# Three edits to a hybrid decoder layer: small column operations moved between engines, a load issued earlier, a sum of squares moved to VectorE

## The chip, the cores and the metric

The kernel runs on one core of one Trainium2 chip. The time is device microseconds of one execution; of several runs the median is taken. A core has a matrix engine (TensorE, PE in the profile, with its weight loads in a row of their own, PEld) and three engines for elementwise work, each with its own stream of instructions that it works off in order: VectorE (DVE), ScalarE (ACT) and GpSimd (POOL). SyncE (SP) issues nearly all DMA transfers here, also in order. PE writes to banks of PSUM; the program lets PE overwrite one only when it has been read.

## The reference

One decoder layer over x of 1024 tokens by 1024 columns, float32. What is computed, in short:

```python
h = rmsnorm(x, norm_g)
proj = h @ w_in     # gla q, k, v, gate, rank-16 code; stick-breaking q, k, v, gate; merge logits
log_a = log_sigmoid(g_rank @ w_dec_up + b_dec) / 16
# gated linear attention, 4 heads, in chunks of 64 tokens
attn = einsum(qe, ke) * mask;  o_intra = attn @ v
o = q_i @ S;  S = d_i[..., None] * S + k_i.T @ v_i        # scan over the chunks
y_a = (rmsnorm(o_gla, gla_norm_g) * silu(g_gate)) @ w_pa
# stick-breaking attention, 8 heads, queries in blocks of 128
A[t, s] = sigmoid(z[t, s]) * prod_{s<j<t} (1 - sigmoid(z[t, j]))
y_b = ((A @ v) * silu(s_gate)) @ w_pb
merged = g_a * y_a + g_b * y_b                            # g = sigmoid(m_logits + b_gate)
x = rmsnorm(x + merged @ w_o, final_g)
```

Both the inputs and the output are float32.

## The kernel before

**Products.** Each float32 operand of a large product is split into a high and a low part (tiles of type fp32r), and a product is made of three matmuls (high by high, low by high, high by low). `split` (L163 to L165) does this: ScalarE copies the high part (L164), VectorE subtracts it from the operand to get the low part (L165). Every large product also follows a scheme with seven block products instead of eight. `pair_job` (L235 on) does so for 256 columns of a weight: POOL makes sums of weight blocks (L243 to L246), `two` and `b22` split them, and the units 0 to 6 (L279 on) run one block product each, 12 matmuls at L269 to L271. After units 0, 2 and 3 `keep` (L275, ScalarE) copies the bank to a tile `f`; after the others an `evict` takes the result of a quarter (J, n): `total` (L308, VectorE) adds the kept tile to the bank. Units 0, 2 and 4 write to one bank in turn, each adding to what stands there, so the next product into it waits for the copy.

**Order of the work.** The program goes through these stages: (1) the start: row blocks of 128 tokens are normed, transposed on PE, and multiplied with the first weights of the values, which come in two halves of 512 rows; (2) the linear-attention values; (3) a list of pair jobs (merge gates, GLA q and k, gates, stick-breaking q, k, values), the later ones interleaved with the gated linear-attention recurrence, four units for each step; (4) stick-breaking attention; (5) the output products and the last norm, row block by row block. Engine orders are set by a scheduler, except within regions under `manual_schedule`, where ScalarE and VectorE follow the order of the code; the start (L483 on) and the last row are of this kind.

**The lines around the change.**

- The start: `norm_a(tb)` (L434) sums the squares of a row block on ScalarE (L438), multiplies by 1/1024 on VectorE (L229) and takes the power -1/2 on POOL (L230). L494 and L499 make the high part `hi0` and the low part `lo0` of the first weight half on VectorE; L500 makes the high part `hi1` of the second on ScalarE. `first_v` multiplies block 0 by them (L222); `turn_x` transposes the next block (L472) and splits it.
- The value pairs: `sv_pair` makes the stick-breaking values with tokens along the free axis. It needs the differences of neighbouring tokens. `vend` (L594) keeps the last token's column of each block of 128; `diff` subtracts 511 columns at once (L602) and the first column by itself, from `vend` of the half before (L604), or as a negation in the first half (L606). `turn` then transposes the differences on PE (L611), splits them and stores them (L615).
- The recurrence: steps are (head, block). `gl_half` loads `qe` and `ke` for four blocks (L894, L895); `gl_load` loads a step's values `vr` (L904) and its gate `g` (L906); `gl_local` makes the step's local attention and splits `vr` into `vh` and `vl`; `gl_gate` transposes the normed output (L970), multiplies by the gate and stores it. The tiles `vr` and `g` have three buffers each.
- The last row block comes in two halves of 256 columns. Each half adds its bank to `y` (L1589); ScalarE squares and sums it (L1591). For the first half the sum is added to that of the other 512 columns (L1595); for the second half both are added and scaled (L1598), POOL takes the power (L1599), and the row is scaled (L1602, L1603) and stored by two queues (L1605, L1606).

Of the kernel before, what the change touches and what calls it, by code (L numbers as in the profile page):

```python
# [9 lines left out]
F32 = mybir.dt.float32  # L10
# [92 lines left out]
def hybrid_layer(ctx: ExitStack, tc: tile.TileContext, x, norm_g, w_in, w_up, b_dec,  # L103
# [306 lines left out]
    with tc.tile_pool(name="p0", bufs=3, reuse_waits="tile") as p0:  # L410
# [70 lines left out]
        with tc.manual_schedule(engines={mybir.EngineType.Activation, mybir.EngineType.DVE}):  # L481
# [13 lines left out]
            keep_warm(WARM[1])  # L495
            for g in range(2):
                nc.vector.tensor_sub(hq[0, g][1][:, :, 0:P], pts[g], hq[0, g][0][:, :, 0:P].bitcast(F32))
            norm_a(1)
            nc.vector.tensor_sub(lo0, raw0, hi0.bitcast(F32))  # L499
            nc.scalar.activation(hi1, raw1, AF.Copy)  # L500
            for g in range(2):
                whole(0, g, pts[g])
# [79 lines left out]
    def sv_pair(i):  # L582


        held = []

        def evict(J, n, bank, add):
            if add is None:
                add = ev.tile([P, HALF], F32, tag="f", name="f")
                nc.scalar.activation(add, bank, AF.Copy)  # L590
            else:
                total(bank, add)
            h = 2 * i + J
            nc.vector.tensor_copy(vend[:, h, 4 * n:4 * n + 4], add[:, P - 1:HALF:P])  # L594
            held.append((J, n, h, add))
            if (J, n) != (1, 1):
                while held:
                    diff(*held.pop())

        def diff(J, n, h, add):  # L600
            d = ev.tile([P, HALF], F32, tag="f", name="f")
            nc.vector.tensor_sub(d[:, 1:HALF], add[:, 0:HALF - 1], add[:, 1:HALF])  # L602
            if n:
                nc.vector.tensor_sub(d[:, 0:1], vend[:, h, 3:4], add[:, 0:1])  # L604
            else:
                nc.vector.tensor_scalar(d[:, 0:1], add[:, 0:1], -1.0, None, op0=ALU.mult)  # L606

            def turn():
                pt = ps.tile([P, HALF], F32, tag="tr", name="tr")
                for b in range(4):  # L610
                    nc.tensor.transpose(pt[:, b * P:(b + 1) * P], d[:, b * P:(b + 1) * P], ident)  # L611
                o = stage()
                split(pt, o[:, 0], o[:, 1])
                for e in range(2):
                    nc.sync.dma_start(d_v[h][:, 4 * n:4 * n + 4, e],  # L615
                                      o[:, e].bitcast(F32).rearrange("p (b c) -> p b c", c=P))

            late.append(turn)

        return pair_job(w_in, C_SV + i * DV, evict)  # L620
# [245 lines left out]
    am = [gv.tile([P, P], F32, tag=f"am{i}", name=f"am{i}", bufs=1) for i in range(2)]  # L866
    for a in am:
        nc.gpsimd.memset(a[CH:P, 0:CH], 0.0)
    gh, ghalf, gblk = {}, {}, {}
    steps = [(h, b) for h in range(GLA_H) for b in range(NT)]  # L870

    def split2(src, shape, tag, bufs=2):
# [16 lines left out]
    def gl_half(h, m):  # L889
# [8 lines left out]
                             .unsqueeze(2).to_broadcast([P, 8, CH]))  # L898
        ghalf[h, m] = {"qe": qe, "q2": q2, "ke": ke}

    def gl_load(h, b):

        v = gv.tile([P, DV], F32, tag="vr", name="vr", bufs=3)
        nc.sync.dma_start(v, d_gv[:, b, h * DV:(h + 1) * DV])  # L904
        g = gv.tile([P, 2, P], F32, tag="g", name="g", bufs=3)
        nc.sync.dma_start(g, d_gg[h][:, :, b * P:(b + 1) * P])  # L906
        gblk[h, b] = {"vr": v, "g": g}
# [70 lines left out]
            nc.sync.dma_start(d_ogl[e][:, :, h, b * P:(b + 1) * P], o[:, :, e].bitcast(F32))  # L978

    gl_half(0, 0)  # L980
    gl_load(*steps[0])
    pairs.run(4)
    gl_load(*steps[1])
# [601 lines left out]
    for i in range(2):  # L1585
# [2 lines left out]
        product(bank, "A22", "T4", 3, i == 1, cs)  # L1588
        nc.vector.tensor_add(y[:, cs], bank[:, cs], y[:, cs])  # L1589
        junk = ps.tile([P, HALF], F32, tag="av", name="junk", bufs=1)  # L1590
        nc.scalar.activation(junk[:, cs], y[:, cs], AF.Square, accum_out=sq[:, i:i + 1])  # L1591
        if i == 0:
            for e in late:
                evict_c(*e)
            nc.vector.tensor_add(sq[:, 2:3], sq[:, 0:1], pre[1, 3][:, 0:1])  # L1595
            nc.vector.tensor_mul(y[:, cs], y[:, cs], fg[:, cs])
        else:
            nc.vector.tensor_scalar(r, sq[:, 1:2], sq[:, 2:3], 1.0 / D, op0=ALU.add, op1=ALU.mult)  # L1598
            nc.gpsimd.tensor_tensor(r, r, nhalf, op=ALU.pow)  # L1599
            nc.vector.tensor_mul(y[:, cs], y[:, cs], fg[:, cs])  # L1600
    cut = 5 * P
# [29 lines left out]
```

## Time and profile before

| what | value |
|---|---|
| median of 3 runs | 1177.04 us (1176.06 to 1178.81) |
| the profiled execution | 1176.68 us, span 1175.0 us |
| mean granted TensorE clock | 0.998 |
| memory read and written | 150.06 MB and 88.08 MB, 203 GB/s over the span |
| PE busy, 0 to 20 us (start) | 16.31 of 20 |
| PE busy, 20 to 280 us (values, first pair jobs) | 260.00 of 260 |
| PE busy, 280 to 300 us (recurrence begins) | 19.30 of 20 |
| PE busy, 300 to 700 us | 399.98 of 400 |
| PE busy, 700 to 720 us (a value pair) | 19.00 of 20 |
| PE busy, 720 to 1160 us | 439.53 of 440 |

A timeline row has the start in us, the duration in us, the engine, the line, the operation, the tile written and the tiles read, their shapes, and in brackets the idle time of the engine before it and what ended that. In a row of groups x is the count, then come the summed busy us and the mean ns of one. In a row of waits stand who waits for whom, and then the summed us of waiting, the number of waits and the longest one. A row of a DMA issue ends with the KB of one transfer and the us from its issue to its landing. In a window row each engine's busy us come in the order PE, PEld, DVE, ACT, POOL, then the granted clock, the DMA share and GB/s.

### The profile page before, as it was taken

What the parts mean: (1) busy time and instruction counts of PE and PEld (TensorE: products, weight loads), DVE (VectorE), ACT (ScalarE), POOL (GpSimd) and SP (SyncE); (2) the same over time, 40 slices, a digit from 0 to 9 for tenths busy, and PEclk for the clock granted to TensorE, in tenths of its full rate; (3) what the DMA queues carried; (4) which work ended last, traced back from release to release, by engine and by line L of the source; (5) the groups of instructions that cost most, each with busy time, mean ns of one, the idle gap of its engine ahead of it and who ended that gap; (6) DMA issues with size and microseconds to landing.
All of it is one profiled execution on the core that took longest, in us unless ns stands there. A gap on an engine that the chain in (4) does not pass through costs nothing.

```text
span 1175.0 us, 16650 instructions
## 1 busy us (share of the span) xinstructions
PE 1162.1 (99%) x5823; PEld 979.5 (83%) x5823; DVE 857.2 (73%) x1441; ACT 558.3 (48%) x1046; POOL 244.3 (21%) x217
## 2 busy tenths in 40 slices
PE   8999999999999999999999999999999999999997
PEld 8999888887888888888888888888888888888886
DVE  6797667888676876776666677457677876488986
ACT  6556663433444545544444343344444444365544
POOL 1022232334242242342242233000000000700001
PEclk9999999999999999999999999999999999999999
DMA  8325549997455665654444357799766656858652
GB/s 290 127 63 162 206 165 327 329 308 241 134 185 180 195 217 162 201 178 133 159 141 131 109 174 237 260 311 337 250 200 216 205 167 195 284 162 286 215 197 108
DMA packets 189456, 239.25 MB, mean 204 GB/s; under 512 B 12438, under 2 KB 128300, under 8 KB 187836
## 3 DMA queue, kind: packets, MB, share of 16 engines
q1 hardware_dynamic: 188796, 237.20, 61.1%
q8 instruction: 46, 0.75, 0.3%
q10 hardware_dynamic: 576, 0.98, 0.2%
q14 instruction: 38, 0.31, 0.1%
HBM read 150.06 MB, written 88.08 MB: 203 GB/s over the span
## 4 chain that ended last, share of the span: by engine, by line
PE 96%; DVE 2%; DMA 1%; ACT 1%; issue 1%; SPq 0%; POOLq 0%; POOL 0%; ACTq 0%; DVEq 0%
PE pp L269 17%; PE pp L270 17%; PE pp L271 17%; PE pp L204 3%; PE pp L205 3%; PE pp L203 3%; PE pp L222 2%; PE av L1108 2%; PE av L1109 2%; PE tr L1086 1%; PE av L1107 1%; PE z L1068 1%; PE z L1070 1%; PE z L1069 1%; PE xa L1363 1%; PE xa L1362 1%
## 5 line engine op out<-in xcount | busy, mean ns | idle before, releaser
L269 PE MATMUL pp<-S,wh 128*128 128x512 f32 x372 | 147.0, 395 | 0.7 <-ACT f L275 0.7
L271 PE MATMUL pp<-S,wl 128*128 128x512 f32 x372 | 145.0, 390 | 0.0
L270 PE MATMUL pp<-S,wh 128*128 128x512 f32 x372 | 144.9, 390 | 0.0
L308 DVE TENSOR_TENSOR f<-pp,f 128x512 f32<-128x512 f32 x93 | 63.9, 687 | 70.2 <-PE pp L271 63.8
L165 DVE TENSOR_TENSOR wl<-tt,wh 128x1024 fp32r<-128x1024 f32 x62 | 75.8, 1222 | 52.6 <-ACT wh L164 52.3
L164 ACT ACTIVATE wh<-tt 128x1024 fp32r<-128x1024 f32 x62 | 65.6, 1059 | 75.0 <-PE pp L270 67.4
L243 POOL TENSOR_TENSOR tt<-raw 128x512 f32<-128x512 f32 x31 | 43.5, 1403 | 258.8 <-DVE wl L165 232.8
L275 ACT ACTIVATE f<-pp 128x512 f32<-128x512 f32 x93 | 55.0, 592 | 79.8 <-PE pp L271 74.2
L1074 DVE TENSOR_TENSOR_SCAN be<-be,m 128x128 f32<-128x128 f32 (+3 forms) x64 | 86.1, 1347 | 3.4 <-ACT be L1071 3.2
L164 ACT ACTIVATE wh<-raw 128x1024 fp32r<-128x1024 f32 (+1 forms) x47 | 48.4, 1030 | 84.0 <-PE pp L270 48.5
L269 PEld LDWEIGHTS pp<-S,wh 128*128 128x128 f32 x372 | 70.5, 190 | 15.1 <-ACT f L275 0.9
L271 PEld LDWEIGHTS pp<-S,wl 128*128 128x128 f32 x372 | 69.8, 188 | 14.8
L270 PEld LDWEIGHTS pp<-S,wh 128*128 128x128 f32 x372 | 69.9, 188 | 13.8
L165 DVE TENSOR_TENSOR wl<-raw,wh 128x1024 fp32r<-128x1024 f32 (+1 forms) x47 | 63.1, 1343 | 18.4 <-ACT wh L164 17.2
L1071 ACT ACTIVATE be<-z 128x384 f32<-128x384 f32 (+4 forms) x96 | 47.2, 494 | 42.7 <-PE z L1070 38.2
L230 POOL TENSOR_TENSOR r<-r,nhalf 128x1 f32<-128x1 f32 x40 | 25.2, 629 | 194.3 <-DVE r L229 194.3
L1268 POOL TENSOR_TENSOR N<-A,A 128x512 f32<-128x512 f32 x4 | 6.6, 1660 | 241.0 <-DMA A<-d_osb 241.0
L269 PE MATMUL pp<-ha11h,wh 128*128 128x512 f32 x124 | 49.2, 397 | 0.0
L269 PE MATMUL pp<-ha12h,wh 128*128 128x512 f32 x124 | 49.0, 395 | 0.0
L164 ACT ACTIVATE dh<-raw 128x512 fp32r<-128x512 f32 x31 | 19.6, 631 | 61.4 <-PE pp L270 61.4
L269 PE MATMUL pp<-ha22h,wh 128*128 128x512 f32 x124 | 48.7, 393 | 0.0
L269 PE MATMUL pp<-S,dh 128*128 128x512 f32 x124 | 48.6, 392 | 0.0
(546 smaller groups left out, 3428.0 us busy)
## 6 DMA issues: line engine op xcount, KB each, us to landing
raw<-in_w_in_dram SPq DMA_DIRECT2D x31, 1024.0 KB, 6.2
d_t<-t SPq DMA_DIRECT2D x16, 512.0 KB, 4.8
d_ogl<-o SPq DMA_DIRECT2D x64, 128.0 KB, 2.4
d_q<-o SPq DMA_DIRECT2D x16, 512.0 KB, 3.3
d_k<-o SPq DMA_DIRECT2D x16, 512.0 KB, 4.8
d_v<-o SPq DMA_DIRECT2D x32, 256.0 KB, 2.3
k<-d_k SPq DMA_DIRECT2D x8, 1024.0 KB, 6.6
v<-d_v SPq DMA_DIRECT2D x16, 512.0 KB, 5.5
```

The costliest lines, as they stand in the source:

```text
L164: nc.scalar.activation(hi, src, AF.Copy)
L165: eng.tensor_sub(lo, src, hi.bitcast(F32))
L203: nc.tensor.matmul(pt, whi[:, kb], h_, start=kb == 0, stop=False)
L204: nc.tensor.matmul(pt, whi[:, kb], l_, start=False, stop=False)
L243: nc.gpsimd.tensor_sub(t1, b[:, 0, 1], b[:, 0, 0])
L269: nc.tensor.matmul(pt, bh[:, j], ah[:, j], start=first and j == 0, stop=False, skip_group_check=True)
L270: nc.tensor.matmul(pt, bh[:, j], al[:, j], start=False, stop=False, skip_group_check=True)
L271: nc.tensor.matmul(pt, bl[:, j], ah[:, j], start=False, stop=j == 3, skip_group_check=True)
L275: nc.scalar.activation(t[nm], t[bank], AF.Copy)
L308: nc.vector.tensor_add(add, bank, add)
L1071: nc.scalar.activation(om[:, off + pc * w:off + (pc + 1) * w], zt[:, 0:w], AF.Sigmoid, scale=-inv_sqrt)
L1074: nc.vector.tensor_tensor_scan(rest, rest, m1[:, off:T][:, ::-1], 1.0, op0=ALU.mult, op1=ALU.max)
```

## The change

Five pieces of code change, in four places.

- In the start the low part `lo0` of the first weight half is computed before `norm_a(1)` instead of behind it.
- In the value pairs the copy into `vend` and the first column of the differences go from VectorE to ScalarE (one activation with scale -1 and a bias in place of the subtraction or the negation).
- In the recurrence a new function, `gl_values`, allocates and loads a step's `vr`; it is called for steps 0 and 1 ahead of the first `gl_load`, which then loads only `g` for those two. Later steps load both as before.
- In the last row the first half's squares stay on ScalarE; its sum is now also multiplied by 1/1024. The second half's squares, their sum, the scaling and the addition of the first part are one call on VectorE, `tensor_tensor_reduce`, in place of the square on ScalarE and the addition on VectorE.

```diff
--- before.py
+++ after.py
@@ -495,8 +495,8 @@
             keep_warm(WARM[1])
             for g in range(2):
                 nc.vector.tensor_sub(hq[0, g][1][:, :, 0:P], pts[g], hq[0, g][0][:, :, 0:P].bitcast(F32))
+            nc.vector.tensor_sub(lo0, raw0, hi0.bitcast(F32))
             norm_a(1)
-            nc.vector.tensor_sub(lo0, raw0, hi0.bitcast(F32))
             nc.scalar.activation(hi1, raw1, AF.Copy)
             for g in range(2):
                 whole(0, g, pts[g])
@@ -591,7 +591,7 @@
             else:
                 total(bank, add)
             h = 2 * i + J
-            nc.vector.tensor_copy(vend[:, h, 4 * n:4 * n + 4], add[:, P - 1:HALF:P])
+            nc.scalar.activation(vend[:, h, 4 * n:4 * n + 4], add[:, P - 1:HALF:P], AF.Copy)
             held.append((J, n, h, add))
             if (J, n) != (1, 1):
                 while held:
@@ -600,10 +600,7 @@
         def diff(J, n, h, add):
             d = ev.tile([P, HALF], F32, tag="f", name="f")
             nc.vector.tensor_sub(d[:, 1:HALF], add[:, 0:HALF - 1], add[:, 1:HALF])
-            if n:
-                nc.vector.tensor_sub(d[:, 0:1], vend[:, h, 3:4], add[:, 0:1])
-            else:
-                nc.vector.tensor_scalar(d[:, 0:1], add[:, 0:1], -1.0, None, op0=ALU.mult)
+            nc.scalar.activation(d[:, 0:1], add[:, 0:1], AF.Identity, scale=-1.0, bias=vend[:, h, 3:4] if n else 0.0)
 
             def turn():
                 pt = ps.tile([P, HALF], F32, tag="tr", name="tr")
@@ -866,7 +863,7 @@
     am = [gv.tile([P, P], F32, tag=f"am{i}", name=f"am{i}", bufs=1) for i in range(2)]
     for a in am:
         nc.gpsimd.memset(a[CH:P, 0:CH], 0.0)
-    gh, ghalf, gblk = {}, {}, {}
+    gh, ghalf, gblk, gvs = {}, {}, {}, {}
     steps = [(h, b) for h in range(GLA_H) for b in range(NT)]
 
     def split2(src, shape, tag, bufs=2):
@@ -898,10 +895,15 @@
                              .unsqueeze(2).to_broadcast([P, 8, CH]))
         ghalf[h, m] = {"qe": qe, "q2": q2, "ke": ke}
 
+    def gl_values(h, b):
+        v = gvs[h, b] = gv.tile([P, DV], F32, tag="vr", name="vr", bufs=3)
+        nc.sync.dma_start(v, d_gv[:, b, h * DV:(h + 1) * DV])
+
     def gl_load(h, b):
 
-        v = gv.tile([P, DV], F32, tag="vr", name="vr", bufs=3)
-        nc.sync.dma_start(v, d_gv[:, b, h * DV:(h + 1) * DV])
+        if (h, b) not in gvs:
+            gl_values(h, b)
+        v = gvs.pop((h, b))
         g = gv.tile([P, 2, P], F32, tag="g", name="g", bufs=3)
         nc.sync.dma_start(g, d_gg[h][:, :, b * P:(b + 1) * P])
         gblk[h, b] = {"vr": v, "g": g}
@@ -978,6 +980,8 @@
             nc.sync.dma_start(d_ogl[e][:, :, h, b * P:(b + 1) * P], o[:, :, e].bitcast(F32))
 
     gl_half(0, 0)
+    for s in range(2):
+        gl_values(*steps[s])
     gl_load(*steps[0])
     pairs.run(4)
     gl_load(*steps[1])
@@ -1588,14 +1592,14 @@
         product(bank, "A22", "T4", 3, i == 1, cs)
         nc.vector.tensor_add(y[:, cs], bank[:, cs], y[:, cs])
         junk = ps.tile([P, HALF], F32, tag="av", name="junk", bufs=1)
-        nc.scalar.activation(junk[:, cs], y[:, cs], AF.Square, accum_out=sq[:, i:i + 1])
         if i == 0:
+            nc.scalar.activation(junk[:, cs], y[:, cs], AF.Square, accum_out=sq[:, 0:1])
             for e in late:
                 evict_c(*e)
-            nc.vector.tensor_add(sq[:, 2:3], sq[:, 0:1], pre[1, 3][:, 0:1])
+            nc.vector.tensor_scalar(sq[:, 2:3], sq[:, 0:1], pre[1, 3][:, 0:1], 1.0 / D, op0=ALU.add, op1=ALU.mult)
             nc.vector.tensor_mul(y[:, cs], y[:, cs], fg[:, cs])
         else:
-            nc.vector.tensor_scalar(r, sq[:, 1:2], sq[:, 2:3], 1.0 / D, op0=ALU.add, op1=ALU.mult)
+            nc.vector.tensor_tensor_reduce(junk[:, cs], y[:, cs], y[:, cs], 1.0 / D, sq[:, 2:3], ALU.mult, ALU.add, r)
             nc.gpsimd.tensor_tensor(r, r, nhalf, op=ALU.pow)
             nc.vector.tensor_mul(y[:, cs], y[:, cs], fg[:, cs])
     cut = 5 * P
```

**ScalarE and SP where the recurrence begins.** First ScalarE before the change; `vh` is the high part of a step's values, `qsh` of its queries, `f` at L275 the copy of a product's bank, `o` at L558 a sigmoid of a gate pair.

```order
L164 ACTIVATE vh_2748<-vr_2654 128x256
L164 ACTIVATE qsh_2815<-q2_2649 128x128
L164 ACTIVATE qsh_2953<-q2_2649 128x128
L275 ACTIVATE f_2675<-pp_2662 128x512
L164 ACTIVATE wh_2702<-raw_2508 128x1024
L558 ACTIVATE o_2698<-f_2675 128x512
L164 ACTIVATE vh_2811<-vr_2735 128x256
L275 ACTIVATE f_2718<-pp_2662 128x512
```

The same stretch of ScalarE after the change:

```order
L164 ACTIVATE vh_2748<-vr_2654 128x256
L164 ACTIVATE qsh_2815<-q2_2649 128x128
L164 ACTIVATE qsh_2953<-q2_2649 128x128
L164 ACTIVATE vh_2811<-vr_2656 128x256
L275 ACTIVATE f_2677<-pp_2664 128x512
L164 ACTIVATE wh_2704<-raw_2508 128x1024
L558 ACTIVATE o_2700<-f_2677 128x512
L275 ACTIVATE f_2720<-pp_2664 128x512
```

The second step's `vh` stood behind the sigmoid and ahead of the second copy; it stands ahead of the first copy now. On SP, the queue of DMA issues, before the change:

```order
L895 DMA ke_2650<-d_gk0_120 128x512
L904 DMA vr_2654<-d_gv_132 128x256
L552 DMA d_gk3_123<-f_2576 128x512
L906 DMA g_2656<-d_gg0_133 128x2x128
L239 DMA raw_2677<-in_w_in_dram 128x8x256
L552 DMA d_gk2_122<-f_2593 128x512
L904 DMA vr_2735<-d_gv_132 128x256
```

And after it:

```order
L900 DMA vr_2654<-d_gv_132 128x256
L552 DMA d_gk3_123<-f_2576 128x512
L900 DMA vr_2656<-d_gv_132 128x256
L908 DMA g_2658<-d_gg0_133 128x2x128
L239 DMA raw_2679<-in_w_in_dram 128x8x256
L552 DMA d_gk2_122<-f_2593 128x512
L908 DMA g_2737<-d_gg0_133 128x2x128
```

The second step's `vr` went from behind the store of `d_gk2` to a place ahead of the first step's `g`.

**VectorE and ScalarE in a value pair**, at the quarter with n = 1. VectorE before the change (`wl` is a weight's low part, `o` the low part of transposed differences):

```order
L165 TENSOR_TENSOR wl_7162<-tt_6703,wh_7161 128x1024
L594 COPY vend_217<-f_7145 128x4
L602 TENSOR_TENSOR f_7148<-f_7145 128x511
L604 TENSOR_TENSOR f_7148<-vend_217,f_7145 128x1
L165 TENSOR_TENSOR o_7156<-tr_7151,o_7156 128x512
```

After it, VectorE has only the 511 columns between the two low parts, and the small operations stand on ScalarE:

```order
L164 ACTIVATE dh_7129<-raw_6701 128x512
L594 ACTIVATE vend_217<-f_7031 128x4
L603 ACTIVATE f_7123<-f_7031 128x1
L603 ACTIVATE f_7126<-f_7056,vend_217 128x1
L164 ACTIVATE wh_7161<-tt_6703 128x1024
L590 ACTIVATE f_7145<-pp_6955 128x512
L164 ACTIVATE o_7156<-tr_7151 128x512
L594 ACTIVATE vend_217<-f_7145 128x4
L603 ACTIVATE f_7148<-f_7145,vend_217 128x1
```

Five small operations stand among ScalarE's copies there that it didn't have before.

**VectorE in the last row.** Before the change:

```order
L1595 TENSOR_TENSOR sq<-sq,pre 128x1
L1596 TENSOR_TENSOR y<-y,fg 128x256
L1589 TENSOR_TENSOR y<-pp,y 128x256
L1598 TENSOR_SCALAR pre<-sq 128x1
L1600 TENSOR_TENSOR y<-y,fg 128x256
```

After it:

```order
L1599 TENSOR_SCALAR sq<-sq,pre 128x1
L1600 TENSOR_TENSOR y<-y,fg 128x256
L1593 TENSOR_TENSOR y<-pp,y 128x256
L1602 ISA junk,pre<-y,sq 128x256
L1602 ISA pre 128x1
L1604 TENSOR_TENSOR y<-y,fg 128x256
```

The one call became two instructions: the fused operation over 256 columns, and one that writes its sum to the column `pre`.

## Prediction

> **What bounds the kernel now.** I read the page's busy times first, then the list of who waited for whom on the matmul engine, then the windows of the end, and only then the timeline around each of its waits.
>
> ```profile
> PE 1162.1 (99%) x5823; PEld 979.5 (83%) x5823; DVE 857.2 (73%) x1441; ACT 558.3 (48%) x1046; POOL 244.3 (21%) x217
> ...
> PE pp L222 <- DVE vw L499: 1.3, 1, 1.3
> PE tr L970 <- DVE o L165: 1.0, 1, 1.0
> PE pp L269 <- ACT f L275: 0.7, 1, 0.7
> ...
> 1160.00:1175.00 15.00, 7.93 (x47) 0.87 0.37 141
> ```
>
> PE is busy for 1162.1 of 1175.0 us, so 12.9 us is all that any change off PE can win. The window row puts 15.00 - 7.93 = 7.07 us of it at the end, where PE has nothing left to do. Three single waits of 1.3, 1.0 and 0.7 us are the largest that the changed lines could touch. The change edits no matrix product, so its gain can only come from these three and from the end: four places, each priced by what ends last there. Outside them VectorE and ScalarE idle more than they are late, and what they save there is worth nothing.
>
> **Place 1, the start.** The low part of the first weight half (L499) is moved ahead of the second row block's statistics (the small L229, which waits for ScalarE).
>
> ```profile
> 10.61 1.28 DVE L499 TENSOR_TENSOR vw<-raw,vw 128x1088 fp32r<-128x1088 f32 x1
> 10.77 1.53 POOL L230 TENSOR_TENSOR r<-r,nhalf 128x1 f32<-128x1 f32 x1 [4.21 <-DVE r L229]
> 11.15 1.11 ACT L500 ACTIVATE vw<-raw 128x1088 fp32r<-128x1088 f32 x1 [0.65 <-DMA raw<-in_w_in_dram]
> 11.94 0.52 PE L222 MATMUL pp<-vw,ha11h 128*128 128x272 f32 x2 [1.28 <-DVE vw L499]
> ...
> 14.16 0.60 ACT L164 ACTIVATE ha11h<-tr 128x512 fp32r<-128x512 f32 x1
> 15.10 0.63 PE L472 MATMUL tr<-ident,xs 128*128 128x128 f32 x4
> ...
> 3.85 7.21 DMA raw<-in_w_in_dram
> ...
> 11.15 1.11 ACT vw L500
> ```
>
> Now L499 starts about 0.6 us earlier, as VectorE idled 0.45 us for ScalarE in front of L229 (0.15 us), and PE can go on at 11.35 instead of 11.94. But it has only four matmuls' work there (0.5 us) before it needs the high part of the second weight half, and that is ScalarE's L500, which starts at 11.15 because a load lands then and ends at 12.26 as before. PE waits again, at 12.30. Behind L500 ScalarE runs without a gap to L164 (14.16 to 14.76), so PE gets the second block's first operand when it did. The second group of transposes moves from 15.10 to about 15.05. This is what the last two rows, from the chain that ended last, say: the chain goes through the load and L500, not through L499. Of 1.3 us of named wait I take **-0.05 us**; the ends are 0 and -0.6 (all of L499's shift kept).
>
> **Place 2, the recurrence's first steps.** The load of the second step's values (vr) is issued where the first step's gate load (g) stood, one DMA after the first values instead of five. Its own cost is none: one DMA moves past a g, a 1 MB weight load and a store on SP's queue, each of which goes out later by the 0.4 to 0.6 us that an issue takes. What counts is that the scheduler also moved its user, the high part vh, ahead of the copy of a product's bank (L275) on ScalarE.
>
> ```profile
> 277.49 0.53 SPq L906 DMA_DIRECT2D g<-d_gg  x1
> 279.88 0.61 SPq L904 DMA_DIRECT2D vr<-d_gv  x1
> 280.68 0.58 ACT L275 ACTIVATE f<-pp 128x512 f32<-128x512 f32 x1
> 281.17 2.68 DVE L165 TENSOR_TENSOR qsl<-q,qsh 128x128 fp32r<-128x128 f32 x2
> 281.91 0.39 PE L269 MATMUL pp<-S,wh 128*128 128x512 f32 x1
> 284.49 0.64 ACT L558 ACTIVATE o<-f 128x512 f32<-128x512 f32 x1 [1.49 <-DVE f L308]
> 287.88 0.42 ACT L164 ACTIVATE vh<-vr 128x256 fp32r<-128x256 f32 x1 [2.75 <-DMA vr<-d_gv]
> 288.20 0.58 ACT L275 ACTIVATE f<-pp 128x512 f32<-128x512 f32 x1
> 288.83 0.50 PE L269 MATMUL pp<-S,wh 128*128 128x512 f32 x1 [0.69 <-ACT f L275]
> ...
> vr<-d_gv SPq DMA_DIRECT2D x1, 128.0 KB, 8.0
> ...
> g<-d_gg SPq DMA_DIRECT2D x1, 128.0 KB, 4.8
> ...
> ke<-d_gk SPq DMA_DIRECT2D x1, 256.0 KB, 3.3
> ```
>
> Before, vr was issued at 279.88, behind the weight load, and took 8.0 us. At 287.88 ScalarE's vh had waited for it, and behind vh stood the copy for which PE waited 0.69 us. That wait goes: with vh done early, this copy follows the sigmoid L558. VectorE gets one more small operation among the two qsl (1.34 us each while POOL is busy), which makes L558 start at about 285.85 and the copy end at 287.0, ahead of the 288.14 at which PE needs it. **What is late next** is the same pattern one product earlier: vh now stands in front of the copy that ran at 280.68, and PE's matmul at 281.91 overwrites the bank that this copy reads. From vh's start to PE's resumption the rows give 288.83 - 287.88 = 0.95 us, so PE waits if vr lands after 281.91 - 0.95 = 280.96, which is 3.5 us behind an issue at 277.49. No row shows a vr load in that place. The nearest are g, of the same size and in that very slot but in shorter pieces (4.8 us: landing 282.29, a wait of 1.33), and ke, issued ahead of it (3.3 us: no wait). I take the middle, 4.05 us: landing 281.54, a wait of 0.58 us in place of 0.69, so **-0.1 us**, with ends -0.7 and +0.65.
>
> **Place 3, the value pairs.** The change takes 16 copies (L594), 8 subtractions (L604) and 8 negations (L606) off VectorE and puts 32 small operations on ScalarE.
>
> ```profile
> L604 DVE TENSOR_TENSOR f<-vend,f 128x1 f32<-128x1 f32 x8 | 3.4, 423 | 0.0
> L164 ACT ACTIVATE qsh<-q 128x128 fp32r<-128x128 f32 x28 | 8.3, 301 | 0.0
> ...
> 701.98 1.73 POOL L243 TENSOR_TENSOR tt<-raw 128x512 f32<-128x512 f32 x1 [7.99 <-DVE wl L165]
> 702.49 1.24 DVE L604 TENSOR_TENSOR f<-vend,f 128x1 f32<-128x1 f32 x1
> 702.78 0.60 PE L611 MATMUL tr<-ident,f 128*128 128x128 f32 x4
> 702.98 0.60 ACT L275 ACTIVATE f<-pp 128x512 f32<-128x512 f32 x1 [1.37 <-PE pp L271]
> 703.65 0.68 DVE L165 TENSOR_TENSOR o<-tr,o 128x512 fp32r<-128x512 f32 x1
> 704.38 0.44 PE L970 MATMUL tr<-ident,on 128*128 128x128 f32 x2 [1.00 <-DVE o L165]
> ```
>
> Here the 1.0 us wait is made. A one-column subtraction took 1.24 us instead of its usual 0.15 because it stood until POOL's L243 was through (701.98 + 1.73 = 703.71, its own end 703.73). The low part L165 behind it released the transposes' bank at 704.33. Without L604 and the copy ahead of it, L165 starts at about 702.45 and ends at 703.15; it reads PSUM, and its 0.68 us at 703.65 lie beside POOL's next operation, so POOL doesn't stretch it. PE's own transposes L611 end at 703.38 and become the bound: **-1.0 us**. ScalarE's price for 32 operations is below 32 x 0.30 = 9.6 us by the 128-column copy; the cover is its waiting for PE, 1.37 us in front of L275 at that very place, where two of them stand (0.6 us). The ends are -1.0 and 0 (the operations on ScalarE delay something that takes the wait's place).
>
> **Place 4, the last row.** The second half's squares go from ScalarE to one VectorE instruction that also sums, scales and adds the rest.
>
> ```profile
> 1168.59 0.42 DVE L1589 TENSOR_TENSOR y<-pp,y 128x256 f32<-128x256 f32 x1
> 1169.17 0.39 ACT L1591 ACTIVATE junk<-y 128x256 f32<-128x256 f32 x1 [0.41 <-DVE y L1589]
> 1169.71 0.21 DVE L1598 TENSOR_SCALAR pre<-sq 128x1 f32<-128x1 f32 x1 [0.71 <-ACT junk L1591]
> 1170.01 0.66 POOL L1599 TENSOR_TENSOR pre<-pre,nhalf 128x1 f32<-128x1 f32 x1 [2.58 <-DVE pre L1598]
> ...
> L954 DVE SCALAR_TENSOR_TENSOR S<-S,fac,pu 128x256 f32<-128x256 f32 x24 | 11.3, 469 | 0.0
> L1521 DVE SCALAR_TENSOR_TENSOR y<-y,pre,fg 128x512 f32<-128x512 f32 x10 | 7.1, 745 | 0.1
> L1074 DVE TENSOR_TENSOR_SCAN be<-be,m 128x256 f32<-128x256 f32 x8 | 5.4, 678 | 0.0
> ```
>
> Before, 1.00 us passed from the sum's end (1169.01) to POOL's start (1170.01), over ScalarE and back. Now it is VectorE alone: a start right behind (0.04), the fused operation, the read of its sum, 0.09 to POOL. No row shows the fused operation. A plain 256-column one takes 0.42, a two-operation one 0.469, the scan 0.678; I take 0.47, the nearest in kind. For the read I take 0.15, a one-column operation. The scaled sum ahead of it is a two-scalar operation (0.21 instead of 0.16) and delays VectorE by 0.06. Together 0.81, so **-0.2 us**; the ends are -0.35 and +0.1.
>
> [...]
>
> **The sum.** -0.05 - 0.1 - 1.0 - 0.2 = -1.35 us. The profiled execution took 1176.68 us (span 1175.0), so 1175.3; the median of the runs shown is 0.36 us higher (1177.04), which gives 1175.7. I say 1175.5.
>
> **The rivals.**
> - *The values come in time.* vr lands within 3.5 us, as ke did, and both waits at 282 and 288 are gone: 0.6 us less, 1174.9. For it: vr has half of g's pieces. Against: g took 4.8 in that slot.
> - *A load takes the place of the wait* (slower). Place 2's mechanism with vr as late as its worst row: 8.0 us behind 277.49 is 285.49, PE stands for 4.5 us at 281.91, 3.85 more than before: 1175.5 + 3.95 = 1179.5. All gains are used up when vr lands later than 282.9 (5.4 us). Against: the weight load no longer stands in front of it.
> - *The fused sum runs at the scan's pace*, 0.68 instead of 0.47, and its read at 0.21: 1175.8. [...]
> - *The wait at 704 stays*, because ScalarE's new columns or something else release the bank late: 1176.5. Against: ScalarE's 1.37 us of idle time there.
> - *The start's shift is kept*: 1174.95, if the load of the second half lands half a microsecond earlier than it did.
>
> **How the numbers follow.** Chances: forecast 0.47, values in time 0.18, fused sum slow 0.13, wait stays 0.11, load late 0.06, start kept 0.05. The range starts at the two faster rivals together with a quick fused sum (1174.2) less a little for the spread of a median, 1173.9; it ends where the wait stays, vr lands like g and the sum is slow (1177.5), 1177.6. It leaves out the late load and some measuring error, about 2 in 10. A difference of 0.2%, 2.35 us, is about what a measurement of this kernel can tell from none. The forecast's 1.35 us lies inside; only the faster rivals with a lucky median reach over it (0.2), only the late load goes past it on the other side (0.06), and 0.74 stays for no difference that can be told.
>
> **What would show it.** Right: PE's list of waits without L970, L499's wait cut to a half and another for ScalarE's vw behind it, a PE wait of up to 1.3 us near 282 for L275 behind vh, none at 288; PE idle down to about 11.5 us. POOL's last power about 0.2 us closer to the last sum. Wrong: a fused operation of 0.7 us; a wait that ScalarE's one-column operations cause between 660 and 750; more than 2 us of PE's wait near 282.

## The result and the profile after

The changed kernel takes 1174.64 us (median of 14 runs, 1174.48 to 1175.11); the kernel before took 1177.0 us beside it. The ratio is 0.9980, 95% interval 0.9973 to 0.9988. One of the 14 executions of the kernel before took 2994.56 us; the median is nearly the same without it (1176.98), and the ratio leaves it out. The change is worth 2.4 us, at the edge of what the prediction called no difference that can be told, and the interval lies clear of 1; predicted were 1175.5 us and a range of 1173.9 to 1177.6. The profiled execution took 1174.77 us with a span of 1173.0 (before: 1176.68 and 1175.0).

| what | before | after |
|---|---|---|
| median | 1177.0 | 1174.64 |
| span of the profiled execution | 1175.0 | 1173.0 |
| PE busy, 280 to 300 us | 19.30 | 20.00 |
| PE busy, 700 to 720 us | 19.00 | 20.00 |

First the page's busy times of the changed kernel and, from the list of who waited for whom, PE's rows that name a changed line. The columns are the summed us, the number of waits and the longest.

```profile
PE 1161.8 (99%) x5823; PEld 978.9 (83%) x5823; DVE 854.6 (73%) x1410; ACT 562.7 (48%) x1076; POOL 241.4 (21%) x217
...
PE pp L222 <- DVE vw L498: 0.7, 1, 0.7
PE pp L222 <- ACT ha12h L164: 0.5, 1, 0.5
...
PE pp L222 <- ACT vw L500: 0.2, 1, 0.2
```

The waits for L970's and L275's releasers are gone, and the start's 1.3 us have become 0.7 and 0.2, with 0.5 behind them where 0.4 stood. VectorE has 31 recorded instructions fewer and ScalarE 30 more; their busy times moved by 2.6 and 4.4 us.

Since PE runs the same matmuls in nearly the same order, each one's start can be compared between the two traces. The difference (after less before) is +0.23 us at the end of the start, -0.49 behind 288 and -0.55 from 295 on, -0.62 behind 662, -1.79 behind 704, and from there to the last product it stays between -1.77 and -1.85. The +0.23 come with a load that landed later in this execution: ScalarE's L500, which waits for it, starts at 11.35 for 11.15. So two of the four places carry nearly all of the gain. These are the recurrence's rows after the change, in the timeline:

```profile
277.84 0.44 SPq L900 DMA_DIRECT2D vr<-d_gv  x1
...
281.23 0.42 ACT L164 ACTIVATE vh<-vr 128x256 fp32r<-128x256 f32 x1
281.55 0.58 ACT L275 ACTIVATE f<-pp 128x512 f32<-128x512 f32 x1
281.92 0.39 PE L271 MATMUL pp<-ha12h,wl 128*128 128x512 f32 x1
282.18 0.50 PE L269 MATMUL pp<-S,wh 128*128 128x512 f32 x1
282.52 0.40 PE L270 MATMUL pp<-S,wh 128*128 128x512 f32 x1
...
286.80 0.58 ACT L275 ACTIVATE f<-pp 128x512 f32<-128x512 f32 x1
```

And the row of that load in the list of DMA issues:

```profile
vr<-d_gv SPq DMA_DIRECT2D x1, 128.0 KB, 3.4
```

The second step's values land 3.4 us behind their issue, at 281.20. ScalarE was free at 281.11 and stood about 0.1 us for them; the list leaves out waits that short, so the row of `vh` names none. The copy behind it ends at 282.13, and PE, which would have gone on at 282.15 (its matmuls stand 0.23 us apart), goes on at 282.18. Nothing was to spare. The second copy ends at 287.4, well ahead of its use.

The value pair, and then the tail, after the change:

```profile
700.88 0.21 ACT L594 ACTIVATE vend<-f 128x4 f32<-128x4 f32 x1
700.98 0.29 ACT L603 ACTIVATE f<-f,vend 128x1 f32<-128x1 f32 x1
701.20 0.68 DVE L602 TENSOR_TENSOR f<-f 128x511 f32<-128x511 f32 x1
701.36 1.66 POOL L243 TENSOR_TENSOR tt<-raw 128x512 f32<-128x512 f32 x1 [7.98 <-DVE wl L165]
701.80 0.68 DVE L165 TENSOR_TENSOR o<-tr,o 128x512 fp32r<-128x512 f32 x1
702.60 0.38 PE L972 MATMUL tr<-ident,on 128*128 128x128 f32 x2
```

```profile
1166.87 0.42 DVE L1593 TENSOR_TENSOR y<-pp,y 128x256 f32<-128x256 f32 x1
1167.32 0.49 DVE L1602 CUSTOM_DVE_ANT_0 junk<-y,sq 128x256 f32<-128x256 f32 x1
1167.73 0.14 DVE L1602 DVE_READ_ACCUMULATOR2_ANT pre<- 128x1 f32 x1
1167.91 0.42 DVE L1604 TENSOR_TENSOR y<-y,fg 128x256 f32<-128x256 f32 x1
1167.95 0.79 POOL L1603 TENSOR_TENSOR pre<-pre,nhalf 128x1 f32<-128x1 f32 x1 [2.30 <-DVE pre L1602]
1168.77 0.55 DVE L1606 TENSOR_SCALAR y<-y,pre 128x640 f32<-128x640 f32 x1 [0.44 <-POOL pre L1603]
```

In the first, the low part L165 starts 0.60 us behind the start of L602, with POOL's sum beside it, and PE's transposes L972 name no wait. In the second, the fused sum takes 0.49 us and the read of it 0.14. From the last addition's end (1167.29) POOL starts after 0.66 us; before it was 1.00.

### The profile page after: what moved, and what is told of

Same layout as the page of the kernel before. It is cut to its first block, busy times and chain, and to the rows that moved or that the text cites. A ratio compares the mean times of both kernels' runs of the same rounds, so it can differ in the third digit from the quotient of the medians.

```text
span 1173.0 us, 16653 instructions
## 1 busy us (share of the span) xinstructions
PE 1161.8 (99%) x5823; PEld 978.9 (83%) x5823; DVE 854.6 (73%) x1410; ACT 562.7 (48%) x1076; POOL 241.4 (21%) x217
## 4 chain that ended last, share of the span: by engine, by line
PE 97%; DVE 1%; DMA 1%; issue 0%; ACT 0%; SPq 0%; POOLq 0%; POOL 0%; ACTq 0%
PE pp L269 17%; PE pp L271 17%; PE pp L270 17%; PE pp L205 3%; PE pp L204 3%; PE pp L203 3%; PE pp L222 2%; PE av L1112 2%; PE av L1113 2%; PE tr L1090 1%; PE av L1111 1%; PE z L1072 1%; PE z L1074 1%; PE z L1073 1%; PE xa L1366 1%; PE xa L1367 1%
## 5 line engine op out<-in xcount | busy, mean ns | idle before, releaser
L165 DVE TENSOR_TENSOR wl<-tt,wh 128x1024 fp32r<-128x1024 f32 x62 | 76.7, 1237 | 52.5 <-ACT wh L164 52.1
L275 ACT ACTIVATE f<-pp 128x512 f32<-128x512 f32 x93 | 55.1, 592 | 77.5 <-PE pp L271 73.9
L165 DVE TENSOR_TENSOR wl<-raw,wh 128x1024 fp32r<-128x1024 f32 (+1 forms) x47 | 63.4, 1349 | 18.4 <-ACT wh L164 17.2
L271 PE MATMUL pp<-ha11h,wl 128*128 128x512 f32 x124 | 48.3, 390 | 0.0
```

The lines of the kernel that those rows point to most:

```text
L165: eng.tensor_sub(lo, src, hi.bitcast(F32))
L271: nc.tensor.matmul(pt, bl[:, j], ah[:, j], start=False, stop=j == 3, skip_group_check=True)
L275: nc.scalar.activation(t[nm], t[bank], AF.Copy)
```

## The experiments

All times below are medians of 11 runs in four groups: the first four kernels, then those with the last row undone, the values behind the gate, the column first and the ends only, then three more, and the last by itself. Only the first group holds the changed kernel too; all others are compared with its 1174.65 there, though they ran on other chips. The kernel before was timed in each group and stood at 1176.72, 1176.78, 1176.87 and 1176.80, so the comparison across groups is uncertain by up to 0.15 us. Line numbers are those of each kernel.

### Each edit undone alone

The changed kernel again, as the base.

> The changed kernel again, on the chip of the three that follow, as what they are compared with. Its runs so far: median 1174.64 us, all between 1174.48 and 1175.11. Expected: 1174.6, within 0.2.

Measured: 1174.65 us (1174.43 to 1174.85), with 1176.72 for the kernel before.

The start's order put back:

```diff
-            nc.vector.tensor_sub(lo0, raw0, hi0.bitcast(F32))
             norm_a(1)
+            nc.vector.tensor_sub(lo0, raw0, hi0.bitcast(F32))
```

> The changed kernel with the start's order put back (low part L499 behind the second block's statistics). Theory (ScalarE's high part of the second half, started by a load, sets the pace): within 0.2 us of the changed kernel; PE's wait for L499 is 1.3 us again, and the waits behind it for ScalarE and for the second block's operand shrink by about as much. Rival (the earlier low part is kept by PE): 0.4 to 0.6 us slower than the changed kernel.

Measured: 1174.63 us (1174.38 to 1176.23). The edit is worth nothing. PE's rows of this kernel's timeline and the ScalarE row that sets them:

```profile
11.24 1.11 ACT L500 ACTIVATE vw<-raw 128x1088 fp32r<-128x1088 f32 x1 [0.67 <-DMA raw<-in_w_in_dram]
12.01 0.52 PE L222 MATMUL pp<-vw,ha11h 128*128 128x272 f32 x2 [1.24 <-DVE vw L499]
...
16.48 0.52 PE L222 MATMUL pp<-vw,ha12h 128*128 128x272 f32 x2 [0.36 <-ACT ha12h L164]
```

And of the changed kernel:

```profile
11.35 1.11 ACT L500 ACTIVATE vw<-raw 128x1088 fp32r<-128x1088 f32 x1 [0.65 <-DMA raw<-in_w_in_dram]
11.54 0.52 PE L222 MATMUL pp<-vw,ha11h 128*128 128x272 f32 x2 [0.68 <-DVE vw L498]
...
12.51 0.52 PE L222 MATMUL pp<-vw,ha11h 128*128 128x272 f32 x2 [0.20 <-ACT vw L500]
...
16.65 0.52 PE L222 MATMUL pp<-vw,ha12h 128*128 128x272 f32 x2 [0.52 <-ACT ha12h L164]
```

From L500's start, which a load sets, to PE's next operand 5.24 us pass with the edit undone and 5.30 with it. The edit moves PE's waits, and its operand comes when it did.

The second step's values loaded where they were before:

```diff
-    for s in range(2):
-        gl_values(*steps[s])
     gl_load(*steps[0])
```

> The changed kernel with the second step's values loaded where they were before. Theory (both of PE's waits are gone, since the values land about 3.4 us after their issue, just in time): 0.7 us slower than the changed kernel in the profiled execution, with PE's 0.7 us wait for L275 back near 288 and the operand stream at 282 without the 0.16 us slip; in the times more than that and a wider spread than 1174.5 to 1175.1, if it is the late load that made the spread of before. Rival (the load gains nothing by itself): within 0.2 us of the changed kernel.

Measured: 1175.18 us (1174.74 to 1175.76), 0.53 above the base, with a spread of 1.0 us against the base's 0.4. The profiled execution was the fastest of the 11, and its list names no wait of PE for L275, against what was expected of it:

```profile
279.85 1.32 SPq L900 DMA_DIRECT2D vr<-d_gv  x1
...
287.27 0.42 ACT L164 ACTIVATE vh<-vr 128x256 fp32r<-128x256 f32 x1 [2.24 <-DMA vr<-d_gv]
287.60 0.58 ACT L275 ACTIVATE f<-pp 128x512 f32<-128x512 f32 x1
```

ScalarE stood for the load here too, but it landed at 287.27 (7.4 us behind its issue), where in the trace of before it landed at 287.88 (8.0 us). With 0.6 us less PE gets its bank almost in time: its matmuls behind 288 slip by 0.18 us against the base, too little for the list. So the wait of 0.7 us was no fixed price: it hangs on that load's landing, which was not the same in the two executions. The other ten runs are up to 1.0 us longer; they left no trace, so that a later landing makes them longer is likely and not shown. The kernel before spread more in the same group (1175.97 to 1178.32 in 33 runs), so the late load doesn't account for all of its spread as far as 11 runs can tell.

The value pairs' small operations back on VectorE, all four of the lines as in the kernel before:

```diff
-            nc.scalar.activation(vend[:, h, 4 * n:4 * n + 4], add[:, P - 1:HALF:P], AF.Copy)
+            nc.vector.tensor_copy(vend[:, h, 4 * n:4 * n + 4], add[:, P - 1:HALF:P])
...
-            nc.scalar.activation(d[:, 0:1], add[:, 0:1], AF.Identity, scale=-1.0, bias=vend[:, h, 3:4] if n else 0.0)
+            if n:
+                nc.vector.tensor_sub(d[:, 0:1], vend[:, h, 3:4], add[:, 0:1])
+            else:
+                nc.vector.tensor_scalar(d[:, 0:1], add[:, 0:1], -1.0, None, op0=ALU.mult)
```

> The changed kernel with the value pairs' small column operations back on VectorE. Theory: 1.2 us slower than the changed kernel; PE waits 1.0 us at the gate's transposes again, and one subtraction of a column takes over 1.2 us beside POOL's sum. Rival (the place is sensitive to when things fall, and the other edits have moved it): the subtraction isn't caught by POOL's operation, PE doesn't wait, within 0.3 us.

Measured: 1175.93 us (1175.86 to 1176.43), 1.28 above the base. The wait is back as it was, rows of its timeline:

```profile
701.38 1.73 POOL L243 TENSOR_TENSOR tt<-raw 128x512 f32<-128x512 f32 x1 [7.98 <-DVE wl L165]
701.89 1.24 DVE L604 TENSOR_TENSOR f<-vend,f 128x1 f32<-128x1 f32 x1
...
703.05 0.68 DVE L165 TENSOR_TENSOR o<-tr,o 128x512 fp32r<-128x512 f32 x1
...
703.79 0.44 PE L975 MATMUL tr<-ident,on 128*128 128x128 f32 x2 [1.00 <-DVE o L165]
```

POOL's sum ends at 703.11, the subtraction of one column at 703.13. PE names 1.00 us, and its matmuls lose 1.23 us there against the base.

The last row as in the kernel before (the square on ScalarE, the sum and scaling as one small operation on VectorE):

```diff
+        nc.scalar.activation(junk[:, cs], y[:, cs], AF.Square, accum_out=sq[:, i:i + 1])
         if i == 0:
-            nc.scalar.activation(junk[:, cs], y[:, cs], AF.Square, accum_out=sq[:, 0:1])
...
-            nc.vector.tensor_scalar(sq[:, 2:3], sq[:, 0:1], pre[1, 3][:, 0:1], 1.0 / D, op0=ALU.add, op1=ALU.mult)
+            nc.vector.tensor_add(sq[:, 2:3], sq[:, 0:1], pre[1, 3][:, 0:1])
...
-            nc.vector.tensor_tensor_reduce(junk[:, cs], y[:, cs], y[:, cs], 1.0 / D, sq[:, 2:3], ALU.mult, ALU.add, r)
+            nc.vector.tensor_scalar(r, sq[:, 1:2], sq[:, 2:3], 1.0 / D, op0=ALU.add, op1=ALU.mult)
```

> The changed kernel with the last row's squares, sum and scaling as before. Theory (place 4 gained about 0.2 us): 0.2 us slower than the changed kernel's 1174.65, at 1174.85; in the trace 1.0 us from the last sum's end to POOL's start instead of 0.66, and POOL's power at 0.66 instead of 0.79. Rival (the earlier power is paid back in full beside VectorE's product): 1174.65.

Measured: 1174.82 us (1174.66 to 1175.02), 0.17 above the base. This fits the 0.2 us; the two ranges overlap, so the size rests on the traces, where the power starts 0.34 us earlier with the fused sum and takes 0.13 us longer (0.79 for 0.66).

The four prices make 0 + 0.53 + 1.28 + 0.17 = 1.98 us, against 1176.72 - 1174.65 = 2.07 for all of them together: within 0.1 us the edits add up.

### What the values' landing decides

The second step's values behind the first step's gate load, and still ahead of the weight load:

```diff
-    for s in range(2):
-        gl_values(*steps[s])
     gl_load(*steps[0])
+    gl_values(*steps[1])
```

> The changed kernel with one difference: the second step's values are issued behind the first step's gate load instead of ahead of it. ScalarE's order is that of the changed kernel, so the matmul near 282 still waits for the copy behind the values. Theory (PE waits from the landing less about 281.2, the changed kernel's landing at 281.2 being just in time): the issue is 0.5 us later, the landing 0.5 to 1.2 us, PE waits as much near 282, and the time is 0.5 to 1.2 us above the changed kernel's 1174.65. Rival (what counts is that the values are asked for ahead of the weight load; the exact place doesn't matter): within 0.2 us.

Measured: 1175.41 us (1174.96 to 1178.54), 0.76 above the base. Rows of its timeline:

```profile
277.86 0.64 SPq L900 DMA_DIRECT2D vr<-d_gv  x1
...
281.72 0.42 ACT L164 ACTIVATE vh<-vr 128x256 fp32r<-128x256 f32 x1 [0.51 <-DMA vr<-d_gv]
...
282.67 0.50 PE L269 MATMUL pp<-S,wh 128*128 128x512 f32 x1 [0.47 <-ACT f L275]
```

ScalarE stands for the load, and PE goes on 0.95 us behind `vh`'s start, as the prediction had worked it out from the wait at 288. The load took 3.8 us and landed at 281.70. The new wait is the one that the forecast had put at place 2, at nearly its size (0.58 us was forecast, 0.47 is named); one place further back in the queue is enough for it. In the traces PE is 0.5 us later behind it than in the base. This variant is, within its spread, as bad as loading the values late.

Both steps' values ahead of the first queries and keys:

```diff
-    gl_half(0, 0)
     for s in range(2):
         gl_values(*steps[s])
+    gl_half(0, 0)
```

> The changed kernel with the first two steps' values issued ahead of the first queries and keys. Theory (the changed kernel's values land with nothing to spare, PE slips 0.16 us at 282): the values land some 3 us earlier relative to their use, the slip is gone, 0.1 to 0.2 us below 1174.65 and no wider spread. Rival (the queries' load, now issued 0.9 us later, or the weight's high part, now behind the values on ScalarE, comes late): a new wait of PE between 281 and 283, slower than 1174.65 by up to 1 us.

Measured: 1174.69 us (1174.51 to 1175.11): no gain, no loss. The values land in good time here (277.62), but POOL's product that waits for the queries starts later and takes 2.08 us instead of 1.04. ScalarE's copy starts at 281.62 for it, as late as in the changed kernel, and PE's matmul follows at 282.25. What set the place was replaced by something equally late. The rival named the queries, but not that they would cost nothing.

### What held the subtraction

The small operations on VectorE (the copies into `vend` too), with the first column ahead of the 511 others:

```diff
+            if n:
+                nc.vector.tensor_sub(d[:, 0:1], vend[:, h, 3:4], add[:, 0:1])
+            else:
+                nc.vector.tensor_scalar(d[:, 0:1], add[:, 0:1], -1.0, None, op0=ALU.mult)
             nc.vector.tensor_sub(d[:, 1:HALF], add[:, 0:HALF - 1], add[:, 1:HALF])
-            nc.scalar.activation(d[:, 0:1], add[:, 0:1], AF.Identity, scale=-1.0, bias=vend[:, h, 3:4] if n else 0.0)
```

> The value pairs' small column operations stay on VectorE, as before the change, but the first column stands ahead of the 511 others instead of behind them; the rest is the changed kernel. Theory (the wait of 1.0 us came from the one-column subtraction being caught while POOL's sum ran, not from VectorE having too much to do): the subtraction is through before POOL's sum begins, PE's wait at the gate's transposes is gone, and the time is within 0.2 us of 1174.65. Rival (VectorE has one or two operations too many there): 1175.9, as with the columns undone.

Measured: 1175.31 us (1175.11 to 1175.47), between the base and the kernel with the columns undone. At 702 the subtraction starts ahead of POOL's sum (701.41 and 701.50) and takes 0.15 us, and PE names no wait: that half of the theory held. The time came back elsewhere, most of it at another quarter, where 0.38 us arise against the base (steps of 0.08 to 0.15 us arise at 662, 703 and 710):

```profile
683.14 1.30 POOL L245 TENSOR_TENSOR tt<-raw 128x512 f32<-128x512 f32 x1
683.75 0.72 DVE L594 COPY vend<-f 128x4 f32<-128x4 f32 x1
...
684.39 0.14 DVE L605 TENSOR_SCALAR f<-f 128x1 f32<-128x1 f32 x1
684.40 1.31 POOL L244 TENSOR_TENSOR tt<-raw,tt 128x512 f32<-128x512 f32 x1
684.45 1.80 DVE L606 TENSOR_TENSOR f<-f 128x511 f32<-128x511 f32 x1
...
686.40 0.63 PE L611 MATMUL tr<-ident,f 128*128 128x128 f32 x4 [0.20 <-DVE f L606]
```

The copy of four columns stands until POOL's sum ends (684.44 and 684.47), and the one-column operation behind it lets POOL's next sum get in first; then the 511 columns stand for that one (1.80 us instead of 0.68), and PE waits for them. In these rows the operation that started first took its usual time (1.30 us on POOL, 0.14 on VectorE) and the other one stood, the four columns as well as the 511.

Only the copies of the last columns on ScalarE, the first columns on VectorE behind the 511 others:

```diff
-            nc.scalar.activation(d[:, 0:1], add[:, 0:1], AF.Identity, scale=-1.0, bias=vend[:, h, 3:4] if n else 0.0)
+            if n:
+                nc.vector.tensor_sub(d[:, 0:1], vend[:, h, 3:4], add[:, 0:1])
+            else:
+                nc.vector.tensor_scalar(d[:, 0:1], add[:, 0:1], -1.0, None, op0=ALU.mult)
```

> The changed kernel with the first columns back on VectorE, behind the 511 others; only the copies of the last columns (vend) stay on ScalarE. Theory: the subtraction is caught by POOL's sum again and ends with it, PE waits 0.9 to 1.0 us, and the time is 1175.8 to 1175.95. Rival (the number of small operations on VectorE matters): about half of the 1.28 us that undoing both cost, 1175.3.

Measured: 1175.79 us (1175.62 to 1175.88). In its trace the subtraction takes 1.23 us again and PE waits 0.93 us. The number of small operations isn't it.

The small operations on VectorE in the old order, with the second source of the one subtraction from the matmul's bank in PSUM (the line is shown against the kernel with the columns undone; the lines that hand the bank on to it are left out):

```diff
-                nc.vector.tensor_sub(d[:, 0:1], vend[:, h, 3:4], add[:, 0:1])
+                nc.vector.tensor_sub(d[:, 0:1], vend[:, h, 3:4], (add if bank is None else bank)[:, 0:1])
```

> The value pairs' small operations on VectorE and in the old order, with one difference: where a quarter needs no addition, the one-column subtraction reads its second source from the matmul's bank in PSUM instead of ScalarE's copy in SBUF; that is the subtraction that was caught near 702. The rest is the changed kernel. Theory (VectorE's operations with all sources in SBUF stand until POOL's running operation ends, those with a source in PSUM don't): the subtraction takes 0.2 us beside POOL's sum, PE doesn't wait near 702, and 1.05 to 1.2 of the 1.28 us that undoing the columns cost are not paid: 1174.65 to 1174.9. Rival (any small operation on VectorE is held beside POOL): 1175.9, a subtraction of over 1 us, PE's wait of 1.0 us.

Measured: 1174.98 us (1174.78 to 1175.06), 0.95 below the kernel with the columns undone and 0.1 above the expected bracket. The same place:

```profile
701.39 1.73 POOL L243 TENSOR_TENSOR tt<-raw 128x512 f32<-128x512 f32 x1 [7.99 <-DVE wl L165]
701.90 0.14 DVE L605 TENSOR_TENSOR f<-vend,pp 128x1 f32<-128x1 f32 x1
701.97 0.68 DVE L165 TENSOR_TENSOR o<-tr,o 128x512 fp32r<-128x512 f32 x1
...
702.71 0.44 PE L976 MATMUL tr<-ident,on 128*128 128x128 f32 x2
```

Same operation, same column, same moment beside the same sum on POOL: 1.24 us with both sources in SBUF, 0.14 us with one of them in PSUM. This settles what held it here: with both sources in SBUF it stood until POOL's sum ended (703.13 and 703.11), and with one in PSUM it was through at 702.04, 1.08 us before that sum's end (703.12).

The four-column copies into `vend` don't fit the count of sources alone. They read one tile in SBUF, and still one of the 16 takes 1.21 us in the kernel before, where the median is 0.17: it starts at 660.16 and stands until POOL's sum ends (661.37 and 661.34). With the column first it stands 1.21 us too, from 659.33 to 660.54, with the end of POOL's sum at 660.51. Why such a copy stands, no run here tries. This kernel stays 0.33 us above the base; in the traces 0.07 us of that arise at 662, behind such a copy, and 0.14 us at 702.

### The same wait at the end

VectorE's last product with the gain, the gain read from PSUM; ScalarE copies it there behind its last scaling (the fused sum writes its squares to the other half of `junk`, not shown):

```diff
+            nc.scalar.activation(junk[:, 2 * P:HALF], fg[:, 2 * P:HALF], AF.Copy)
...
-            nc.vector.tensor_mul(y[:, cs], y[:, cs], fg[:, cs])
+            nc.vector.tensor_mul(y[:, cs], y[:, cs], junk[:, cs])
```

> The changed kernel with the last product on VectorE, that with the final gain (256 columns, 0.42 us), reading the gain from PSUM, where ScalarE has copied it while it was idle. Theory (the same exclusion works the other way: POOL's last power took 0.79 us, because it stood beside a product with two sources in SBUF): the power takes 0.55 us, the final scaling starts 0.24 us earlier relative to the sum, and the time is 0.2 us below the changed kernel's 1174.65. Rival (a power takes 0.6 to 0.8 there whatever VectorE reads, for instance because of where its own start falls): 1174.65.

Measured: 1174.85 us (1174.62 to 1175.25). POOL's last power took 0.55 us, as the theory says, but the fused sum stood 0.54 us for the copy on ScalarE. So the gain was lost ahead of it. The copy one step earlier:

```diff
+            nc.scalar.activation(junk[:, 2 * P:HALF], fg[:, 2 * P:HALF], AF.Copy)
             for e in late:
                 evict_c(*e)
-            nc.scalar.activation(junk[:, 2 * P:HALF], fg[:, 2 * P:HALF], AF.Copy)
```

> As the run with the gain read from PSUM, but ScalarE copies it ahead of its last scaling (at about 1166.3) instead of behind that scaling's store. Theory (in that run the power took 0.55 us as predicted, and the 0.24 us gained were lost because the fused sum stood 0.5 us for the copy): the fused sum starts right behind the addition, the power takes 0.55 us, the final scaling starts 0.24 us earlier relative to the last addition than in the changed kernel, and the time is 1174.4. Rival (the store of the row block's other half, issued 0.35 us later, ends last): 1174.65 or more.

Measured: 1174.55 us (1174.37 to 1174.77). Rows of its timeline:

```profile
1166.92 0.42 DVE L1593 TENSOR_TENSOR y<-pp,y 128x256 f32<-128x256 f32 x1
1167.49 0.49 DVE L1603 CUSTOM_DVE_ANT_0 junk<-y,sq 128x256 f32<-128x256 f32 x1 [0.15 <-ACT yd L1550]
...
1168.07 0.42 DVE L1605 TENSOR_TENSOR y<-y,junk 128x256 f32<-128x256 f32 x1
1168.12 0.55 POOL L1604 TENSOR_TENSOR pre<-pre,nhalf 128x1 f32<-128x1 f32 x1 [2.41 <-DVE pre L1603]
1168.70 0.55 DVE L1607 TENSOR_SCALAR y<-y,pre 128x640 f32<-128x640 f32 x1 [0.21 <-POOL pre L1604]
```

The power is at 0.55 beside the product, but the fused sum still stands 0.15 us for ScalarE, now for the scaling that the copy pushed back. From the last addition's start to the final scaling 1.78 us pass instead of 1.90. Half of the 0.24 us is kept; the median is 0.1 us lower, which the ranges of the runs do not separate from the base. It is the lowest median of all the kernels here, and no more can be said for it.

## Why the prediction was right, and where its sizes were off

The time lay in the range, 0.9 us below the forecast, and every place behaved by the mechanism that was named for it, though at place 2 the rival came true and not the likeliest case.

**Place 1, the start, -0.05 us.** Right: no difference was measured (1174.63 against 1174.65). The chain of waits had said that the path goes through the load and ScalarE's L500, and with the edit undone PE gets the same operand equally late. The 1.3 us of named wait were worth nothing.

**Place 2, the recurrence, -0.1 us.** The mechanism held, the size didn't. PE does wait when `vr` lands later than about 281 (0.47 us are named with a landing at 281.70), and 0.95 us pass from `vh`'s start to PE's next matmul (seen again with the values behind the gate). But the term took the middle of two nearest rows, 4.05 us for the load, and it took 3.4: nearer to `ke` (3.3) than to `g` (4.8). That is the rival "the values come in time", all but a slip of about 0.2 us at 282. The two traces of the changed kernel gained 0.78 and 0.74 us there against the kernel before (in the first from +0.23 to -0.55), the times 0.53. One thing the prediction did not have: the late load landed 8.0 us behind its issue in one execution and 7.4 in another, so the row of one execution was a sample.

**Place 3, the value pairs, -1.0 us.** Right in mechanism; 1.28 us measured. PE's matmuls moved by 1.17 us at 704, not by the 1.00 us that the wait named, and by 0.07 us at 662, where a copy into `vend` had stood 1.21 us. The first difference is a matter of reading, below. ScalarE's 32 operations are named by no wait of PE, as was said; they take 0.19 to 0.29 us each.

**Place 4, the last row, -0.2 us.** Right: 0.17 by the times and 0.34 less 0.13 by the traces. The fused sum took 0.49 us (0.47 had been taken) and its read 0.14 (0.15). It did not run at the scan's pace, 0.68: it is nearer to the plain 256-column product behind it, which took 0.42. The 0.13 us that POOL gave back were not in the sum.

**The sum**, -1.35 us, was 0.7 us short of the 2.07 measured beside it on one chip: 0.4 us from place 2, 0.28 from place 3. The rest of the 0.9 us by which the forecast lay too high goes with its starting point: 1175.5 and 1.35 make 1176.85, and the kernel before took 1176.72 in that group.

**The chances.** 0.74 had been set on no difference that can be told, by a bound of 0.2%. The 95% interval came out 0.15% wide in all: half of that is less than even the forecast's 1.35 us, 0.11%. So smaller differences can be told here than that bound said.

**A wait of PE costs more than its row says.** Three matmuls of the kernel before that run without a wait:

```profile
281.68 0.39 PE L271 MATMUL pp<-ha12h,wl 128*128 128x512 f32 x1
281.91 0.39 PE L269 MATMUL pp<-S,wh 128*128 128x512 f32 x1
282.14 0.39 PE L270 MATMUL pp<-S,wh 128*128 128x512 f32 x1
```

They are listed with 0.39 us each and start 0.23 us apart. A wait's row counts from the listed end, so 0.16 us of a delay stay unnamed in such a stream. The two traces agree. At 288 the transpose ahead of the wait is listed with 0.33 us, and in the changed kernel the next matmul starts 0.09 us behind its start: 0.24 us are unnamed, 0.69 are named, and 0.94 were gained. At 704 it is listed with 0.27, the next would start 0.11 behind it: 0.16 unnamed, 1.00 named, 1.17 gained. And at 282 of the changed kernel there is a slip of 0.16 us without any wait in the list. That PE was idle for 12.9 us was therefore no upper bound on what a change can win.

## What to carry to other kernels

Where VectorE and POOL both work from SBUF, a tiny VectorE operation can cost as much as what is left of POOL's (1.24 us for one column here): look in the trace for short shapes with long durations, and move them to ScalarE (0.29 us for that column) or, where they have two sources in SBUF, give them one in PSUM (0.14 us), rather than reorder them (0.66 us above the base here). A load's duration from one trace is a sample (8.0 us in one execution here, 7.4 in another): if it lands close to its use by that measure, compare several runs, since its landing may be both the wait and the spread. And add the overlap of PE's matmuls ahead of a wait, duration less spacing (0.39 less 0.23 us here), to the wait before pricing what it is worth.

## What the runs showed of the hardware that was not expected

VectorE and POOL held each other up in more rows than the subtraction's: 511 columns took 1.80 us instead of 0.68 (with the column first), POOL's last power 0.79 instead of 0.55 (the changed kernel against the gain read from PSUM), its product 2.08 instead of 1.04 (with the values first), and a four-column copy 1.21 us instead of 0.16 (the kernel before, at 660.16 and 701.82), though it has one source. The power at the start, in a row that the prediction shows (10.77), is of the same kind: it took 1.53 us beside VectorE's L499 and takes 0.55 in the changed kernel, at 11.63. There and in the last row, before and after, the power ends 0.41 us behind the end of VectorE's operation. A one-column scaling with a single source was not held: in the kernel before it took 0.14 us at 685.81, in the middle of a sum on POOL (from 685.22, 1.82 us). The same 128 KB load took 3.4 us two places ahead of a 1 MB weight load, 3.8 us one place ahead, and 7.4 and 8.0 us behind it and a store; whether either of the two delayed it was not tried apart.
